# A backbone block on one core: the Strassen sums of the second feed-forward weights made in the loop over f and kept in DRAM

## The chip, the cores and the metric

The kernel runs on one core of a Trainium2 chip. The metric is the device time of one execution in microseconds (us), the median of several runs. A profile of one execution gives the start and duration of every instruction on each engine: TensorE (PE for matmuls, PEld for weight loads), VectorE (DVE), ScalarE (ACT), GpSimd (POOL), and SyncE (SP), which issues nearly all DMA transfers.

## The reference

One transformer-like block for a latent stream x of 1024 tokens and 1024 channels, with a context of 256 tokens: modulation, an input projection, four mixers side by side, an output projection, a residual with layer norm, and then a feed-forward network with its own residual and layer norm. Only the feed-forward network matters here, with D = 1024 and D_FF = 2816:

```python
def swiglu(h, w_in, w_out):
    g, u = jnp.split(h @ w_in, 2, axis=-1)
    return (jax.nn.silu(g) * u) @ w_out
...
        x = layer_norm(ALPHA * x + g2 * swiglu(x * (1.0 + sc2) + sh2, w_ffn_in[l], w_ffn_out[l]), ln2_w[l], ln2_b[l])
```

All data are float32. `w_ffn_out`, 2816 x 1024, holds "the second feed-forward weights".

## The kernel before, in words

**Precision.** An operand of a matmul is split into two parts: a high part, which ScalarE makes by a cast (L853), and a low part, which VectorE makes by subtracting the high part from the value (L854, both in `split2`, called with high priority). Each product is the sum of three matmuls: high by high, high by low, low by high (`PASSES`).

**Strassen.** Both feed-forward matmuls are done by Strassen's scheme in Winograd's form: each matrix is cut into 2 x 2 quarters named 11, 12, 21 and 22, and seven products of quarters, or of sums of quarters called T1 to T4, replace eight. For the second weights T2 = 22 - 12 + 11, T1 = 22 - T2 = 12 - 11, T3 = T2 - 11 = 22 - 12 and T4 = 21 - T2.

**First stage: the loop over f (L1424).** The hidden units come in 22 blocks of 128 (`NFF`). After two passes done without Strassen, nine passes with f = 4, 6, ..., 20 make two blocks each. A pass (`gate_up2`) is two Strassen products: one for the gate, whose results ScalarE puts through SiLU into the tile s, and one for the up projection, whose results VectorE multiplies into s. Each `strassen` loads two 512 KB pieces of first weights into the tiles `raw`, makes the sums of their halves (`a_sums`, L1313) and the parts into tiles `whl`, and runs seven products of 12 matmuls (L1344). VectorE reads and adds the results from PSUM (L1349). At the end of a pass `spill` makes four sums of the quarters of s in a tile S (L1400 to L1403) and stores s and S, 1 MB each, into the DRAM tensor `gd` (L1404, L1405).

**Second stage: seven products over `gd` and the second weights.** For each of the products "11", T2, "21", T1, "22", T3 and T4, in this order, `operands` (L1458) loads chunks of two blocks of 128 rows (the last has one): 512 KB of `gd` into a tile `whl`, and what `weights` (L1442) gives. For "11", "21" and "22" that is one load of 512 KB into `raw`. For T2 it is three loads (two into `raw`, one into `whl`) and two VectorE subtractions or additions of 128x1024 (L1450, L1451); the result stays on chip in three pages for the rest of the kernel. For T1, T3 and T4 it is one load and one subtraction with the kept T2 (L1455). Then both operands are split into high and low parts in tiles that `ring` hands out, and 24 matmuls per chunk run (L1476), 132 in a product. VectorE folds the finished products into the residual rows (L1490 to L1501); T4 accumulates into the PSUM banks that hold T3, after T3 has been read. The rows' last layer norm (`ln2`) and the stores of the output follow.

**Buffers.** `page` is a pool of nine tiles of 8 KB per partition. In the loop over f two of them hold rows of the residual, two the quarter "11" of the first stage's input and two its T4; the others pass between s and S. `page3` is a second pool of eight such tiles. `raw` has two buffers, `whl` four. `ring` gives one chunk in five two tiles of `page` and the other four chunks tiles of `page3`.

**Order of the work.** The code is written as a plain program; a planner at compile time orders the instructions of each engine and of SP's queue by a model of their costs, lets work run ahead when its buffers are free, and prefers what is marked as high priority. At run time each engine and the queue keep that order, and an instruction that waits holds up those behind it.

Of the kernel before, what the change touches and what calls it, by code (L numbers as in the profile page):

```python
# [9 lines left out]
F32 = mybir.dt.float32  # L10
# [4 lines left out]
MUL, ADD, SUB, MAX, MIN = ALU.mult, ALU.add, ALU.subtract, ALU.max, ALU.min  # L15
# [692 lines left out]
NFF = DFF // 128  # L708
# [12 lines left out]
def layout(x):  # L721

    f = np.ascontiguousarray
    g = {n: f(x[n]) for n in ("x", "w_mod", "b_mod", "ln1_w", "ln1_b", "ln2_w", "ln2_b", "mlstm_gate_bias", "s5_glu_w")}
    g["cst"] = const_table()
    kp = lambda a: a.reshape(-1, 128).T
    g["cols"] = f(np.concatenate([kp(x["c"]), kp(x["c_ctx"])] + [kp(x[src][0])[:, k0:k0 + nk] for _, src, k0, nk in VEC], 1))

    st = lambda a: a[0].reshape(2, 8, 2, 64).transpose(2, 3, 0, 1).reshape(128, 16)
    ldt = np.broadcast_to(x["s5_log_dt"][0][:, :, None], (2, 16, 64))[None]  # L730
    bt = [x["s5_b_" + n][0].reshape(8, 2, 64, 16).transpose(1, 2, 0, 3).reshape(128, 128) for n in ("re", "im")]
    ct = [x["s5_c_" + n][0].reshape(8, 2, 16, 64).transpose(1, 3, 0, 2).reshape(128, 128) for n in ("re", "im")]
    dk = np.zeros((128, 8), np.float32)
    dk[0:32] = x["s5_d"][0].reshape(8, 32).T
    g["s5p"] = f(np.concatenate([st(x["s5_a_re"]), st(x["s5_a_im"]), st(ldt)] + bt + ct + [dk], 1))
    g["conv_t"] = f(x["conv_w"][0].reshape(31, 2, 128).transpose(2, 1, 0))
    g["sgu_wt"] = f(x["sgu_w"][0].transpose(2, 0, 1))
    g["sgu_bb"] = f(np.repeat(x["sgu_b"][0].reshape(2, 2, 128).transpose(1, 0, 2), 64, 0))
    g["xt"], g["ct"] = (f(x[n][0].T.reshape(8, 128, -1).transpose(1, 0, 2)) for n in ("x", "ctx"))
    tile_ = lambda w: w.reshape(-1, 128, w.shape[1]).transpose(1, 0, 2)  # L740
    half = lambda w: f(np.stack([tile_(w[0:512]), tile_(w[512:1024])]))
    wi = x["w_in"][0]
    g["wt"] = f(np.stack([tile_(wi[:, c:c + 128]) for _, c in TCOLS]))
    g["wk"], g["wb"] = half(wi[:, 256:512]), half(wi[:, 1296:1552])
    g["wv"] = half(np.concatenate([wi[:, 512:768], wi[:, 1024:1040]], 1))
    g["wm"] = f(x["w_mod"][0][:, 0:2 * D].reshape(4, 2, 128, 2, 2, 512).transpose(4, 0, 2, 1, 3, 5))
    blocks = lambda w: f(w.reshape(8, 128, -1, 128).transpose(2, 1, 0, 3))
    g["w1"] = blocks(x["w_ffn_in"][0])
    g["wo"] = f(x["w_out"][0].reshape(4, 2, 128, 2, 512).transpose(3, 0, 2, 1, 4))
    g["w2"] = f(x["w_ffn_out"][0].reshape(NFF // 2, 2, 128, 2, 512).transpose(1, 3, 2, 0, 4).reshape(4, 128, NFF // 2, 512))  # L750
    return g


# [8 lines left out]
def body(tc, A, out):  # L762
    nc = tc.nc
    v, a, pe, gp = nc.vector, nc.scalar, nc.tensor, nc.gpsimd
    e = Env()
    e.nc, e.tc = nc, tc
    st = ExitStack()
    with st:
# [607 lines left out]
            add(o, u2, W_)  # L1376
            use(1, 0, o)

        def gate_up2(f, B, s):
            def gate(i, h, c):  # L1380
                a.activation(s[:, i, h], c, AF.Silu)

            def up(i, h, c):
                v.tensor_tensor(s[:, i, h], c, s[:, i, h], op=MUL)

            def slot(i, h, spare):
                return pg3.tile([128, 512], F32, name="c12", tag="c12", bufs=1) if spare is None else spare

            strassen(f, B, lambda i, h, spare: s[:, i, h], None, gate)
            strassen(NFF + f, B, slot, None, up)  # L1390

        gd = e.dram.tile([8, 128, NFF // 2, 512], F32, name="gd", bufs=1)

        def spill(f, s):
            k = f // 2
# [24 lines left out]
        next(sums)  # L1423
        for f in range(4, NFF, 2):  # L1424
            s = pair()
            gate_up2(f, B, s)
            spill(f, s)


        NK = NFF // 2  # L1430
        ring = itertools.cycle((page, page3, page3, page3, page3))
        T2 = []

        def w2load(q, k, n, tag="raw"):
            r = sg.tile([128, n, 512], F32, name=tag, tag=tag, bufs=2 if tag == "raw" else 4)
            ld(r, A["w2"][q, :, k:k + n])
            return r

        def t2(k, n):
            return T2[k // 4][:, k % 4:k % 4 + n]  # L1440

        def weights(b, k, n):  # L1442

            if b in ("11", "21", "22"):
                return w2load(("11", "12", "21", "22").index(b), k, n)
            if b == "T2":
                if k % 4 == 0:
                    T2.append(page([128, 4, 512]))
                r, x, y = w2load(3, k, n), w2load(1, k, n), w2load(0, k, n, "whl")
                v.tensor_tensor(r, r, x, op=SUB)  # L1450
                v.tensor_tensor(t2(k, n), r, y, op=ADD)  # L1451
                return t2(k, n)
            r = w2load({"T1": 3, "T3": 0, "T4": 2}[b], k, n)
            x, y = (t2(k, n), r) if b == "T3" else (r, t2(k, n))
            v.tensor_tensor(r, x, y, op=SUB)  # L1455
            return r

        def operands(m, b, k, n):  # L1458
# [120 lines left out]
```

## Time and profile before

| | |
|---|---|
| runs | 1181.01 to 1181.26 us, median 1181.09 of 3 |
| profiled execution | 1180.17 us, its span 1177.6 us |
| mean granted TensorE clock | 0.988 |
| TensorE busy with matmuls | 1135.1 us, 96% of the span |
| VectorE busy | 936.4 us, 80% |
| ScalarE busy | 447.6 us, 38% |
| moved by DMA | 160.57 MB, 136 GB/s over the span |
| second stage, first to last matmul | 945.16 to some 1166.7 us |

Times in the rows are microseconds from the start of the span. A row of a timeline or of the chain of waits gives start, duration, engine, line and operation; in brackets stands how long the engine was idle before it and what ended that. A row of a group gives the count after "x", then the busy time, the mean of one in ns, and the idle time ahead with what ended it. A matmul's duration overlaps the next one's, so the pace is read from starts.

### The profile page before, as it was taken

How to read it: one execution, taken by the hardware profiler on the slowest of the kernel's cores; microseconds unless marked ns; L12 is line 12 of the kernel's file. 1: busy time of each engine (PE TensorE's matmuls, PEld its weight loads, DVE VectorE, ACT ScalarE, POOL GpSimd, SP SyncE). 2: the span in 40 equal slices, each digit the busy share in tenths (PEclk: the TensorE clock that was granted, in tenths of full speed). 3: DMA queues.
4: the chain of work that ended last, by engine and by line, in shares of the span. 5: the costliest groups of instructions: out<-in, count | busy, mean ns of one | idle time of the engine just before them, and what ended most of it. 6: DMA issues, size and time to landing. Idle time of an engine off the chain costs nothing.

```text
span 1177.6 us, 15237 instructions
## 1 busy us (share of the span) xinstructions
PE 1135.1 (96%) x5671; PEld 897.8 (76%) x5671; DVE 936.4 (80%) x1837; ACT 447.6 (38%) x691; POOL 9.6 (1%) x30
## 2 busy tenths in 40 slices
PE   6999999999999999999999999999999989999996
PEld 1487788667888778778887888888888877788875
DVE  7588999988899799889867667675767565897996
ACT  1554444522426334582233333233323242533532
POOL 0010000000000000000000000000000000000000
PEclk9999999999999899999999999999999999999998
DMA  9542111021243346353233143413343387867451
GB/s 361 209 136 84 43 46 57 27 77 63 64 133 109 122 145 199 118 204 108 72 107 122 58 141 110 143 60 119 107 143 106 122 292 266 288 205 275 160 180 71
DMA packets 57484, 160.57 MB, mean 136 GB/s; under 512 B 5378, under 2 KB 9634, under 8 KB 57027
## 3 DMA queue, kind: packets, MB, share of 16 engines
q1 hardware_dynamic: 56994, 158.62, 39.6%
q8 instruction: 44, 0.72, 0.2%
q0 software_dynamic: 272, 0.70, 0.2%
q10 hardware_dynamic: 144, 0.29, 0.1%
q14 instruction: 30, 0.24, 0.1%
HBM read 130.77 MB, written 28.82 MB: 136 GB/s over the span
## 4 chain that ended last, share of the span: by engine, by line
PE 70%; DVE 14%; DMA 9%; issue 3%; ACT 3%; SPq 1%; POOL 0%; DVEq 0%; ACTq 0%; POOLq 0%
PE mm L1344 16%; PE mm L883 12%; PE a L1344 8%; PE mm L1183 5%; PE b L1344 4%; PE b L883 4%; PE a L1476 3%; PE mm L892 3%; DMA raw<-in_w_dram 3%; DMA whl<-gd 3%; PE b L1476 2%; DVE pg L854 2%; PE mm L1476 2%; PE b L564 1%; DVE whl L854 1%
## 5 line engine op out<-in xcount | busy, mean ns | idle before, releaser
L853 ACT CAST whl<-raw 128x512 fp32r<-128x512 f32 (+1 forms) x198 | 121.7, 622 | 279.7 <-PE mm L883 67.2
L883 PE MATMUL mm<-pg,whl 128*128 128x512 f32 x816 | 216.7, 404 | 1.6 <-ACT pg L1206 1.2
L1344 PE MATMUL mm<-pg,whl 128*128 128x512 f32 x864 | 204.8, 389 | 0.0
L1344 PEld LDWEIGHTS mm<-pg,whl 128*128 128x128 f32 x864 | 162.1, 188 | 33.8
L854 DVE TENSOR_TENSOR whl<-raw,whl 128x512 fp32r<-128x512 f32 (+1 forms) x198 | 135.6, 691 | 61.1 <-ACT whl L853 59.2
L883 PEld LDWEIGHTS mm<-pg,whl 128*128 128x128 f32 x816 | 146.5, 188 | 39.3 <-issue 6.1
L1344 PE MATMUL a<-pg,whl 128*128 128x512 f32 x432 | 104.3, 390 | 0.6 <-ACT whl L853 0.6
L1344 PEld LDWEIGHTS a<-pg,whl 128*128 128x128 f32 x432 | 80.9, 188 | 18.2 <-ACT whl L853 1.1
L853 ACT CAST pg<-raw 128x1024 fp32r<-128x1024 f32 (+1 forms) x46 | 45.6, 993 | 78.0 <-DVE raw L1455 44.2
L1476 PE MATMUL a<-pg,pg 128*128 128x512 f32 x210 | 63.6, 399 | 3.6 <-DVE hs L1490 2.3
L854 DVE TENSOR_TENSOR pg<-raw,pg 128x1024 fp32r<-128x1024 f32 (+1 forms) x46 | 52.9, 1153 | 16.4 <-ACT pg L853 16.2
L1476 PE MATMUL mm<-pg,pg 128*128 128x512 f32 x234 | 65.7, 389 | 0.0
L892 PE MATMUL mm<-whl,pg 128*128 128x256 f32 (+1 forms) x448 | 63.1, 288 | 0.0
L1476 PE MATMUL b<-pg,pg 128*128 128x512 f32 x210 | 61.6, 389 | 0.0
L892 PEld LDWEIGHTS mm<-whl,pg 128*128 128x128 f32 x448 | 58.1, 190 | 1.5 <-issue 1.1
L853 ACT CAST pg<-whl 128x1024 fp32r<-128x1024 f32 (+1 forms) x42 | 40.9, 977 | 30.7 <-DMA whl<-gd 28.4
L854 DVE TENSOR_TENSOR pg<-whl,pg 128x1024 fp32r<-128x1024 f32 (+1 forms) x42 | 47.3, 1132 | 6.2 <-ACT pg L853 6.1
L1344 PE MATMUL b<-pg,whl 128*128 128x512 f32 x216 | 51.9, 389 | 0.0
L1476 PEld LDWEIGHTS mm<-pg,pg 128*128 128x128 f32 x234 | 43.9, 188 | 9.1
L1183 PE MATMUL mm<-whl,pg 128*128 128x512 f32 x192 | 50.3, 398 | 0.3 <-DVE pg L1171 0.3
L1183 PE MATMUL mm<-pg 128*128 128x512 f32 x192 | 50.4, 406 | 0.1
L1476 PEld LDWEIGHTS a<-pg,pg 128*128 128x128 f32 x210 | 40.4, 193 | 12.9 <-issue 2.7
(471 smaller groups left out, 1810.2 us busy)
## 6 DMA issues: line engine op xcount, KB each, us to landing
raw<-in_w_dram SPq DMA_DIRECT2D x84, 512.0 KB
gd<-pg SPq DMA_DIRECT2D x22, 1024.0 KB
whl<-gd SPq DMA_DIRECT2D x35, 512.0 KB
pg<-in_wm_dram SPq DMA_DIRECT2D x16, 512.0 KB
raw<-in_wo_dram SPq DMA_DIRECT2D x16, 512.0 KB
raw<-in_wt_dram SPq DMA_DIRECT2D x14, 512.0 KB
mw<-in_w_mod_dram SPq DMA_DIRECT2D x24, 256.0 KB
vx<-in_w_mod_dram SPq DMA_DIRECT2D x24, 256.0 KB
```

Of the source, the lines that this page charges most:

```text
L564: pe.matmul(ps[:, x * 65:(x + 1) * 65], lhsT=D[d][:, x], rhs=vx[:, h, :], start=True, stop=True)
L853: a.copy(hi, r)
L854: v.tensor_tensor(lo, r, hi.bitcast(F32), op=SUB)
L883: pe.matmul(ps[h], lhsT=W(wi, k), rhs=rhs(hi, h, k), **f)
L892: pe.matmul(ps, lhsT=lhs(hi, k), rhs=Ws[k // 4](wi, k % 4), start=(k == 0 and n == 0), stop=(k == 7 and n == 2))
L1183: pe.matmul(ps, lhsT=Yr(hi, half, k)[:, t * 128:(t + 1) * 128], rhs=Ws[k // 2](wi, k % 2), start=(i + n == 0), stop=(i == 7 and n == 2))
L1344: pe.matmul(ps, lhsT=W[:, wi, k, :], rhs=B[b][hi][:, k], start=(first and k + n == 0), stop=(k == 3 and n == 2), skip_group_check=True)
L1476: pe.matmul(ps[t], lhsT=Ag[:, hi, k, t * 128:(t + 1) * 128], rhs=Bg[:, wi, k], start=(first and k0 + k + m == 0), stop=(k0 + k == NK - 1 a ...
```

## The change

The sums of the second weights are no longer made in the second stage. A new input layout `w2k` holds the four quarters of one block k side by side, and `w2_sums(k)` loads them (1 MB) into a page X, makes T3, T1, T2 and T4 from them by four VectorE instructions on 128x512, and stores them (1 MB) into a new DRAM tensor `td`. `gate_up2` calls it between its two halves: for block k = f/2 - 2 in each pass, and in the last two passes (f = 18 and f = 20) also for block k = f/2, which makes eleven blocks. In the second stage `weights` becomes one load for every product, from `td` for T1 to T4 and from `w2` for the others; the three pages of T2, the two extra loads and all subtractions there are gone, and the ring gives two chunks in five tiles of `page`.

```diff
+    g["w2k"] = f(x["w_ffn_out"][0].reshape(NFF // 2, 2, 128, 2, 512).transpose(0, 2, 1, 3, 4).reshape(NFF // 2, 128, 4, 512))
...
-        def gate_up2(f, B, s):
+        def gate_up2(f, B, s, between):
...
             strassen(f, B, lambda i, h, spare: s[:, i, h], None, gate)
+            between()
             strassen(NFF + f, B, slot, None, up)
...
+        td = e.dram.tile([4, 128, NFF // 2, 512], F32, name="td", bufs=1)
+
+        def w2_sums(k):
+            X = page([128, 4, 512])
+            ld(X, A["w2k"][k])
+            v.tensor_tensor(X[:, 3], X[:, 3], X[:, 1], op=SUB)
+            v.tensor_tensor(X[:, 1], X[:, 1], X[:, 0], op=SUB)
+            v.tensor_tensor(X[:, 0], X[:, 3], X[:, 0], op=ADD)
+            v.tensor_tensor(X[:, 2], X[:, 2], X[:, 0], op=SUB)
+            ld(td[:, :, k].rearrange("m p c -> p m c"), X)
...
-            gate_up2(f, B, s)
+            gate_up2(f, B, s, lambda: [w2_sums(k) for k in ((f // 2 - 2,) if f < NFF - 4 else (f // 2 - 2, f // 2))])
...
-        ring = itertools.cycle((page, page3, page3, page3, page3))
-        T2 = []
+        ring = itertools.cycle((page, page3, page, page3, page3))
...
         def weights(b, k, n):
-            if b in ("11", "21", "22"):
-                return w2load(("11", "12", "21", "22").index(b), k, n)
-            if b == "T2":
-                if k % 4 == 0:
-                    T2.append(page([128, 4, 512]))
-                r, x, y = w2load(3, k, n), w2load(1, k, n), w2load(0, k, n, "whl")
-                v.tensor_tensor(r, r, x, op=SUB)
-                v.tensor_tensor(t2(k, n), r, y, op=ADD)
-                return t2(k, n)
-            r = w2load({"T1": 3, "T3": 0, "T4": 2}[b], k, n)
-            x, y = (t2(k, n), r) if b == "T3" else (r, t2(k, n))
-            v.tensor_tensor(r, x, y, op=SUB)
+            r = sg.tile([128, n, 512], F32, name="raw", tag="raw")
+            src = td[("T2", "T1", "T4", "T3").index(b)] if b[0] == "T" else A["w2"][("11", "12", "21", "22").index(b)]
+            ld(r, src[:, k:k + n])
             return r
```

More of the change, by code (lines that the diff above doesn't have):

```diff
@@ L1425, in body @@
             s = pair()
-            gate_up2(f, B, s)
+            gate_up2(f, B, s, lambda: [w2_sums(k) for k in ((f // 2 - 2,) if f < NFF - 4 else (f // 2 - 2, f // 2))])
             spill(f, s)
         NK = NFF // 2
-        ring = itertools.cycle((page, page3, page3, page3, page3))
-        T2 = []
[L1434 to L1440, printed above, removed]
-        def weights(b, k, n):
-            if b in ("11", "21", "22"):
-                return w2load(("11", "12", "21", "22").index(b), k, n)
-            if b == "T2":
-                if k % 4 == 0:
-                    T2.append(page([128, 4, 512]))
-                r, x, y = w2load(3, k, n), w2load(1, k, n), w2load(0, k, n, "whl")
-                v.tensor_tensor(r, r, x, op=SUB)
-                v.tensor_tensor(t2(k, n), r, y, op=ADD)
-                return t2(k, n)
-            r = w2load({"T1": 3, "T3": 0, "T4": 2}[b], k, n)
-            x, y = (t2(k, n), r) if b == "T3" else (r, t2(k, n))
-            v.tensor_tensor(r, x, y, op=SUB)
+        ring = itertools.cycle((page, page3, page, page3, page3))
+        def weights(b, k, n):
+            r = sg.tile([128, n, 512], F32, name="raw", tag="raw")
+            src = td[("T2", "T1", "T4", "T3").index(b)] if b[0] == "T" else A["w2"][("11", "12", "21", "22").index(b)]
+            ld(r, src[:, k:k + n])
             return r
```

## The prediction

> **What bounds the kernel now.** I read the page's first rows, then the busy time by stretches over the loop on f and over each product behind it, then TensorE's timeline around the stretches in which it is not full, and last the chain of waits there.
>
> ```profile
> span 1177.6 us, 15237 instructions
> PE 1135.1 (96%) x5671; PEld 897.8 (76%) x5671; DVE 936.4 (80%) x1837; ACT 447.6 (38%) x691; POOL 9.6 (1%) x30
> ```
>
> TensorE is the bound, so the change can only be worth what TensorE loses in the stages that it touches. In the next fence (stretch, length, busy time with count of PE, PEld, DVE, ACT and POOL, granted clock, DMA share, GB/s) the first row is one pass of the loop over f.
>
> ```profile
> 705.00:743.00 38.00, 38.00 (x169) 31.46 (x169) 25.94 (x40) 12.18 (x20) 0.00 (x0) 1.00 0.31 110
> ...
> 942.00:945.20 3.20, 0.04 (x1) 0.04 (x1) 2.90 (x4) 3.20 (x5) 0.00 (x0) 0.99 0.59 197
> 945.20:950.00 4.80, 4.80 (x14) 3.88 (x15) 4.80 (x7) 0.86 (x1) 0.00 (x0) 0.65 0.84 289
> ...
> 976.00:1012.00 36.00, 32.25 (x134) 25.83 (x133) 21.92 (x22) 13.14 (x16) 0.00 (x0) 0.95 0.81 273
> 1012.00:1042.00 30.00, 30.00 (x134) 24.84 (x133) 27.09 (x30) 14.21 (x15) 0.00 (x0) 1.00 0.82 279
> ...
> 995.00:999.70 4.70, 4.70 (x22) 3.85 (x21) 1.86 (x2) 0.46 (x1) 0.00 (x0) 1.00 0.83 289
> 999.70:1002.80 3.10, 0.65 (x4) 0.20 (x2) 2.50 (x4) 1.63 (x2) 0.00 (x0) 1.00 0.55 156
> 1002.80:1007.30 4.50, 4.50 (x13) 3.56 (x14) 3.76 (x5) 1.36 (x2) 0.00 (x0) 0.62 0.93 320
> ...
> 1132.00:1134.90 2.90, 0.58 (x4) 0.19 (x2) 2.01 (x3) 1.80 (x2) 0.00 (x0) 1.00 0.13 52
> 1134.90:1140.60 5.70, 5.70 (x18) 4.57 (x19) 5.70 (x13) 0.00 (x0) 0.00 (x0) 0.70 0.29 95
> 1140.60:1166.70 26.10, 26.08 (x115) 21.23 (x114) 19.69 (x32) 9.37 (x15) 0.00 (x0) 1.00 0.15 51
> 1166.70:1177.60 10.90, 0.00 (x0) 0.00 (x0) 6.30 (x13) 1.44 (x3) 0.00 (x0) 0.67 0.37 144
> ```
>
> The loop over f keeps TensorE full: nothing can be gained there, only lost. The second stage starts at 945; it holds 7 products of 132 matmuls. At full rate 12 matmuls take 2.72 us (the 849.38 row further on), 0.2267 each, so a product takes 29.92 us. The product that reads "21" (1012 to 1042) runs at that rate; the one that reads T2 (976 to 1012) does not, and the first part of T4 (1134.90 to 1140.60) does not. TensorE's own rows give the exact edges:
>
> ```profile
> 945.16 1.65 PE L1476 MATMUL mm<-pg 128*128 128x512 f32 x3 [3.31 <-ACT pg L853]
> ...
> 976.78 0.62 PE L1476 MATMUL a<-pg,pg 128*128 128x512 f32 x2
> ...
> 994.56 0.74 PE L1476 MATMUL a<-pg,pg 128*128 128x512 f32 x2 [1.30 <-ACT pg L853]
> ...
> 1002.79 0.91 PE L1476 MATMUL a<-pg 128*128 128x512 f32 x2 [2.45 <-ACT pg L853]
> ...
> 1012.70 0.84 PE L1476 MATMUL mm<-pg,pg 128*128 128x512 f32 x3
> ...
> 1131.93 0.61 PE L1476 MATMUL b<-pg 128*128 128x512 f32 x2
> 1134.86 5.73 PE L1476 MATMUL a<-pg,pg 128*128 128x512 f32 x17 [2.32 <-DVE hs L1490]
> ```
>
> **What the change removes: the T2 product.** It runs from 976.78 to 1012.70, 35.92 us, and loses 35.92 - 29.92 = 6.0 us: waits of 1.30 and 2.45 us, and a slow restart, 13 matmuls in 4.50 us where 4.50 / 0.2267 = 19.9 fit (6.9 x 0.2267 = 1.55 us; the clock in that row is 0.62). The chain of waits says what was late:
>
> ```profile
> 985.14 5.64 DMA raw<-in_w_dram
> 990.88 1.24 DVE raw L1450
> 992.15 1.24 DVE pg L1451
> ```
>
> A chunk of two k-blocks takes both raw buffers (w22 and w12), 5.64 + 1.24 + 1.24 = 8.1 us before they can be filled again, while TensorE eats a chunk in 24 x 0.2267 = 5.44 us. It also takes two of the four whl buffers (the operand and w11), so the operand's own load comes late as well. Four loads of 512 KB per 5.44 us would be 385 GB/s, and 320 GB/s at a DMA share of 0.93 is what the 1002.80 row reached. After the change a chunk has two loads, one raw buffer and one whl buffer, and no subtraction: load, cast and low part, about 8 us over two raw buffers, 4 us a chunk against 5.44, at 193 GB/s. That is the traffic of the products "11", "21" and "22" now, and "21" loses nothing. I take back all 6.0 us. Bounds: the two waits without the slow restart, 3.75 us; above, 6.0.
>
> **The subtractions of T1, T3, T4.** The groups of the second stage:
>
> ```profile
> L1455 DVE TENSOR_TENSOR raw<-raw,pg 128x1024 f32<-128x1024 f32 (+1 forms) x12 | 13.4, 1132 | 1.8 <-DMA raw<-in_w_dram 1.8
> L1450 DVE TENSOR_TENSOR raw<-raw 128x1024 f32<-128x1024 f32 (+1 forms) x6 | 6.8, 1136 | 10.9 <-DMA raw<-in_w_dram 10.9
> L1451 DVE TENSOR_TENSOR pg<-raw,whl 128x1024 f32<-128x1024 f32 (+1 forms) x6 | 6.8, 1136 | 1.2 <-DMA whl<-in_w_dram 1.1
> L1455 DVE TENSOR_TENSOR raw<-pg,raw 128x1024 f32<-128x1024 f32 (+1 forms) x6 | 6.7, 1133 | 1.6 <-DMA raw<-in_w_dram 1.6
> ```
>
> VectorE loses 13.4 + 6.8 + 6.8 + 6.7 = 33.7 us of work here. It is worth nothing where TensorE is full, which is everywhere but at the start of T4:
>
> ```profile
> 1130.64 1.15 DVE raw L1455
> 1131.81 1.06 ACT pg L853
> ...
> 1132.89 1.23 DVE L854 TENSOR_TENSOR pg<-raw,pg 128x1024 fp32r<-128x1024 f32 x1 [1.11 <-ACT pg L853]
> 1134.03 1.28 DVE L1490 TENSOR_TENSOR hs<-a,g 128x512 f32<-128x512 f32 x2
> ```
>
> T4 adds into the banks that T3 filled, so TensorE waits until VectorE has read the first of them (L1490, 1134.03). The last matmul of T3 starts at 1131.93 + 0.23; the reading stands behind a low part (1132.89) that waited for a cast, which waited for a T4 subtraction (L1455). With 6.7 us of T3's and half of the 13.4 us (T4's) gone, T4's first operand is done earlier and the reading starts as T3 ends. Of the hole, 1134.86 - (1131.93 + 2 x 0.2267) = 2.48 us, I leave 1.0 (one reading of 0.69 and the hand-over) and take 1.5. The restart then stays fast, as after the 1.30 us wait at 994.56 (22 matmuls in 4.70 us, full rate): the slow one costs 25.1 - 18 = 7.1 matmuls, 1.6 us. Together 3.1 us; bounds 0 (the reading is queued as now) and 2.48 + 1.6 = 4.1.
>
> The Trainium skill, TensorE: Matmul & The Clock Gate, section HAM oscillation, has the clock drop only after idle gaps of over about 3.4 us. Here the clock is 0.62 and 0.70 behind waits of 2.45 and 2.32 us, so the trace disagrees. By the page those slow restarts would not be the gaps' doing and could stay, which is a rival below.
>
> **What it adds: one block of sums in each of nine passes, two in the last two.** Per block one load and one store of 1 MB and four VectorE instructions on 128x512. The rows that price them, with those that show the slack in a pass (the second product of its up half starts at 849.38, so that half at 849.38 - 2.72 = 846.66, and the gate half, 7 products of 2.72 us earlier, at 827.62):
>
> ```profile
> 834.69 21.92 SPq L845 DMA_DIRECT2D raw<-in_w_dram  x4
> ...
> 836.40 0.59 ACT L1381 ACTIVATE pg<-mm 128x512 f32<-128x512 f32 x1
> ...
> 841.59 0.69 DVE L1323 TENSOR_TENSOR raw<-raw 128x512 f32<-128x512 f32 x1 [1.00 <-DMA raw<-in_w_dram]
> ...
> 844.24 0.69 DVE L854 TENSOR_TENSOR whl<-raw,whl 128x512 fp32r<-128x512 f32 x1 [0.77 <-ACT whl L853]
> ...
> 849.38 2.72 PE a L1344 x12
> ...
> raw<-in_w_dram SPq DMA_DIRECT2D x84, 512.0 KB
> gd<-pg SPq DMA_DIRECT2D x22, 1024.0 KB
> ```
>
> VectorE: 4 x 0.69 = 2.8 us on 25.94 of 38, that is 28.7; in the last two passes 5.5, 31.4. It fits beside TensorE. DMA: a pass moves 38 x 110 = 4.2 MB now and 6.3 after, 165 GB/s, half of the 320 above. If this cover were gone, all eleven blocks would be 30 us of VectorE and 11 x 2 x 3.3 = 72 us of transfers (1 MB at 320 GB/s is 3.3 us).
>
> The block's first instruction waits for its load, and VectorE works in order: behind it stand the reading of the banks and the low parts of the next weights. SP issues in order too: behind the block's load, which waits for a page, stand the raw loads of the next half. The weights of the second product of the up half are ready at 844.24 + 0.69 = 844.93 and used at 849.38: 4.45 us of slack. The raw loads go out at 834.69; the pass's s page is first written at 836.40, and the block's page is asked for behind it. So I put the block's load behind those raw loads and its store, some 12 us on, ahead of the next pair: 3.3 us late, within 4.45. Pages: nine, of which two hold rows of the residual, two "11", two T4; s, S and the block share three, and each is stored a pass before it is needed. I take 0.5 us for the loop. Bounds: 0 (TensorE is full, so no gain), and both transfers ahead of one pair of loads in each pass: 6.6 - 4.45 = 2.15 us x 9 = 19.
>
> The Trainium skill, DMA: Bandwidth & Descriptors, says (Queues, rings and completion order) that descriptors of one issuing engine are consumed in ring order on each DMA engine, and (Bandwidth) that 1 MB took 6.15 us in its own measurement. With that figure one transfer ahead of the raw loads would already be 6.15 - 4.45 = 1.7 us late, an estimate of 15 us over nine passes; the 320 GB/s of this trace speaks for 3.3 us.
>
> **The start of the stage and the ring.** The wait of 3.31 us at 945.16 and the slow restart behind it (14 matmuls where 21 fit, 1.6 us) stay: the first operands are loaded into the same buffers. The ring now takes pages for two chunks of five, which the freed T2 pages pay for. 0, with bounds of -3 (VectorE is busy there, 2.90 of 3.20 us, but not by T2) and +6.6 (two blocks' stores ahead of the first loads). The last 10.9 us, behind the last matmul, don't change.
>
> **Sum.** -6.0 - 3.1 + 0.5 + 0 = -8.6 us. The profiled execution took 1180.17 us, 2.6 outside its span of 1177.6, and the median of the runs is 0.92 above it. 1181.09 - 8.6 = 1172.5 us.
>
> **Rivals.** (a) The T4 hole stays: the reading is still behind some low part, since the ring lets operands be prepared further ahead. Then -6.0 + 0.5: 1175.6 us. For it: that VectorE is 100% busy in 1134.90 to 1140.60; against: 33.7 us less work. 0.14. (b) The slow restarts are not the gaps' doing and stay (the page's rule): -(6.0 - 1.55) - 1.5 + 0.5 = -5.45, 1175.6 us. Against it: full rate after 1.30 us, slow after 2.32, 2.45 and 3.31. 0.04. (c) The gain moves to the start: the last pass has two blocks, 4 MB more, just ahead of the first operands, and the first wait grows by 6.6 us: 1179.1 us, no change that can be told. For it: a DMA share of 0.84 from 945.20 to 950; against: the last pass starts at 827.62 + 2 x 38.08 = 903.8, its blocks' loads go out some 9 us on, and with 6.6 us of loads, 5.5 of sums and 6.6 of stores (overlapped) they are stored near 930, while the first operands are cast after 941. 0.11. (d) Slower: the loop over f stalls. The block's load gets in front of the raw loads in SP's queue, or VectorE sits on it, in each pass; from 0.95 us a pass on (8.6 / 9) the gain is gone; at 2.15 us it is 1172.5 - 0.5 + 19 = 1191 us. For it: a wait for raw data of 1.00 us at 841.59 shows loads landing later than their place in VectorE's order allows for; against: 4.45 us of slack and 0.31 DMA share. 0.17. (e) More: VectorE is also freer at the start, the first wait shrinks by 3: 1169.5 us. 0.06.
>
> **Chances.** The forecast has 0.48, so faster is 0.48 + 0.14 + 0.04 + 0.06 = 0.72, no change (within 0.2%, 2.4 us, about what a measurement of this kernel can tell) 0.11, slower 0.17. The range reaches from 1167 (T4's upper bound and (e)) to 1186 (three quarters of (d)'s loss); the forecast's own is 1169 to 1176.
>
> **What would show it.** Right: no wait over 1 us in the product that reads T2, its 132 matmuls in 30 us; under 1.3 us of hole at T4 and clock 1.00 behind it; every pass of the loop still 38.1 us; some 34 us less VectorE work behind the loop and 30 more in it. Wrong: waits of matmuls on L1344 for weights or raw loads in the passes (d), a first wait well over 3.31 us (c), a hole at T4 of 2 us or more (a), or slow stretches without a gap ahead of them (b).

## The result and the profile after

The changed kernel takes 1174.44 us (median of 10 runs, 1167.60 to 1178.07); the kernel before, run beside it on the same chip, takes 1181.17 us (10 runs, 1177.87 to 1185.86). The ratio is 0.9942, with a 95% interval of 0.9920 to 0.9963, so the change is worth 4.4 to 9.4 us. The forecast was 1172.5 us, and the measured median lies within its own range of 1169 to 1176. The profiled execution took 1174.02 us (before: 1180.17).

The page's first two lines, and then the busy time by stretches, with the columns of the prediction (stretch, length, PE, PEld, DVE, ACT, POOL, granted clock, DMA share, GB/s):

```profile
span 1172.2 us, 15295 instructions
...
PE 1133.1 (97%) x5671; PEld 895.4 (76%) x5671; DVE 930.0 (79%) x1851; ACT 445.6 (38%) x691; POOL 9.6 (1%) x30
```

```profile
870.00:908.00 38.00, 36.81 (x163) 30.05 (x162) 29.42 (x47) 11.15 (x20) 0.00 (x0) 1.00 0.59 221
...
980.00:1010.00 30.00, 30.00 (x135) 24.82 (x134) 19.72 (x19) 18.33 (x23) 0.00 (x0) 1.00 0.89 314
...
1130.80:1136.50 5.70, 5.70 (x25) 4.73 (x26) 4.65 (x12) 0.00 (x0) 0.00 (x0) 1.00 0.14 55
```

The first row covers a pass of the loop with two blocks: TensorE is no longer full there (36.81 of 38). The second is the product that reads T2: full. The last is the start of T4: 25 matmuls where 18 ran before, at clock 1.00 where 0.70 was granted. TensorE's own rows after the change give the edges:

```profile
891.23 0.73 PE L1345 MATMUL a<-pg,whl 128*128 128x512 f32 x2 [1.19 <-ACT whl L854]
...
950.08 0.96 PE L1470 MATMUL mm<-pg 128*128 128x512 f32 x3 [2.53 <-ACT pg L854]
...
980.75 0.62 PE L1470 MATMUL a<-pg,pg 128*128 128x512 f32 x2
...
1010.67 0.84 PE L1470 MATMUL mm<-pg 128*128 128x512 f32 x3
...
1129.90 0.61 PE L1470 MATMUL b<-pg 128*128 128x512 f32 x2
1130.76 2.97 PE L1470 MATMUL a<-pg,pg 128*128 128x512 f32 x12 [0.25 <-DVE hs L1484]
```

The T2 product runs from 980.75 to 1010.67, 29.92 us: 132 matmuls at full rate. At T4, 1130.76 - (1129.90 + 2 x 0.2267) leaves a hole of 0.41 us. New are waits of 1.19 us for casts of first weights in the up halves of the last two passes of the loop (the other one at 930.86).

The loss of a stretch, here and below, is the distance between two starts less 0.2267 us for each matmul between them. By stages, from the starts of TensorE's matmuls in the profiled executions (the loop is counted from its first product to the first matmul of the second stage, so the wait ahead of that matmul is in it; the second stage is counted to the start of its last row, of three matmuls):

| us | ahead of the loop | loop | second stage |
|---|---|---|---|
| before | 591.67 | 347.49 | 220.68 |
| after | 592.92 | 351.25 | 210.01 |
| difference | +1.25 | +3.76 | -10.67 |

Ahead of the loop nothing was changed, and this stretch lies between 590.0 and 595.9 us in the profiled executions of all kernels here; its 1.25 us is no effect. The three differences, +0.40 behind the last matmul and -0.09 ahead of the first one make the 5.35 us between the two spans. So the second stage gave more than was expected of it (-6.0 - 3.1 = -9.1) and the loop took more than the +0.5.

Why the loop loses begins in SP's queue. First a pass with one block, then one with two (L846 loads the raw first weights, L1403 the block):

```profile
798.68 0.35 SPq L846 DMA_DIRECT2D raw<-in_w_dram  x1
799.08 0.91 SPq L1403 DMA_DIRECT2D pg<-in_w2k_dram  x1
801.40 0.33 SPq L846 DMA_DIRECT2D raw<-in_w_dram  x1
...
875.89 0.34 SPq L846 DMA_DIRECT2D raw<-in_w_dram  x1
876.28 2.79 SPq L1403 DMA_DIRECT2D pg<-in_w2k_dram  x2
879.18 0.41 SPq L846 DMA_DIRECT2D raw<-in_w_dram  x1
```

The block's load stands between the two raw loads of the up half, not behind them as the prediction had it (in the first pass it leaves ahead of both, at 609.46 against 612.66). In the kernel before, the second raw load of a pass leaves 2.1 to 2.7 us behind the first, first pass aside; the prediction's row at 834.69 counts four loads together and hides that gap. VectorE's rows of the same two passes (L1404 to L1407 are the block's four sums, L1324 and L1325 the sums of the raw weights, L855 their low parts):

```profile
807.17 0.69 DVE L1404 TENSOR_TENSOR pg<-pg 128x512 f32<-128x512 f32 x1 [1.06 <-DMA pg<-in_w2k_dram]
...
809.70 0.68 DVE L1324 TENSOR_TENSOR raw<-raw 128x512 f32<-128x512 f32 x1
...
812.35 1.90 DVE L855 TENSOR_TENSOR whl<-raw,whl 128x512 fp32r<-128x512 f32 x3 [0.17 <-ACT whl L854]
...
883.00 0.69 DVE L1404 TENSOR_TENSOR pg<-pg 128x512 f32<-128x512 f32 x1 [0.40 <-DMA pg<-in_w2k_dram]
...
888.57 0.68 DVE L1324 TENSOR_TENSOR raw<-raw 128x512 f32<-128x512 f32 x1
```

The block's data land first, so its sums are placed ahead of the raw weights' sums. With one block the first low part is done at 812.35 + 0.69 = 813.04, and the product that reads it begins at 813.38:

```profile
813.38 2.88 PE L1345 MATMUL a<-pg,whl 128*128 128x512 f32 x12
```

Of the 4.45 us of slack some 0.3 are left: one block just fits. With two, six sums run ahead of L1324 (two more follow it), and TensorE waits.

The traces' semaphore events tell when the second raw load has landed, counted here from the issue of the first one and without the first pass: 6.1 to 7.0 us in the kernel before, 8.4 to 9.5 with one block between the two, 10.8 and 12.1 with two. VectorE starts L1324 0.1 us behind that landing in the kernel before, and 1.1 to 2.0 us behind it in the changed kernel. So the loop's loss has two parts: the transfers make the raw data late, and VectorE's order adds to it.

### The profile page after: what moved, and what is told of

Read it like the earlier page. It is cut to its first block, busy times and chain, and to the rows that moved or that the text cites. A ratio compares the mean times of both kernels' runs of the same rounds, so it can differ in the third digit from the quotient of the medians.

```text
span 1172.2 us, 15295 instructions
## 1 busy us (share of the span) xinstructions
PE 1133.1 (97%) x5671; PEld 895.4 (76%) x5671; DVE 930.0 (79%) x1851; ACT 445.6 (38%) x691; POOL 9.6 (1%) x30
## 4 chain that ended last, share of the span: by engine, by line
PE 77%; DVE 13%; DMA 4%; issue 4%; ACT 2%; POOL 0%; DVEq 0%; ACTq 0%; POOLq 0%
PE mm L1345 16%; PE mm L884 13%; PE a L1345 8%; PE mm L1470 6%; PE mm L1184 4%; PE b L1345 4%; PE b L884 4%; PE a L1470 3%; PE b L1470 3%; PE mm L893 3%; PE c L1470 2%; PE b L564 1%; DVE whl L855 1%; DVE pg L855 1%; DMA raw<-in_w_dram 1%
## 5 line engine op out<-in xcount | busy, mean ns | idle before, releaser
L855 DVE TENSOR_TENSOR whl<-raw,whl 128x512 fp32r<-128x512 f32 (+1 forms) x198 | 133.6, 689 | 46.3 <-ACT whl L854 44.7
L855 DVE TENSOR_TENSOR pg<-raw,pg 128x1024 fp32r<-128x1024 f32 (+1 forms) x52 | 59.6, 1149 | 20.8 <-ACT pg L854 20.7
L855 DVE TENSOR_TENSOR pg<-whl,pg 128x1024 fp32r<-128x1024 f32 (+1 forms) x42 | 47.4, 1133 | 31.9 <-ACT pg L854 31.6
L854 ACT CAST pg<-raw 128x1024 fp32r<-128x1024 f32 (+1 forms) x52 | 51.5, 992 | 48.9 <-DMA raw<-in_w_dram 18.0
L1470 PE MATMUL mm<-pg,pg 128*128 128x512 f32 x171 | 48.0, 389 | 0.0
L1470 PE MATMUL a<-pg,pg 128*128 128x512 f32 x162 | 47.2, 390 | 0.2 <-DVE hs L1484 0.2
L1470 PE MATMUL b<-pg,pg 128*128 128x512 f32 x162 | 47.1, 389 | 0.0
L1345 PEld LDWEIGHTS b<-pg,whl 128*128 128x128 f32 x216 | 40.5, 188 | 8.4
L1184 PEld LDWEIGHTS mm<-pg 128*128 128x128 f32 x192 | 37.4, 198 | 8.6 <-DVE pg L855 0.7
```

The source lines that it names most:

```text
L854: a.copy(hi, r)
L855: v.tensor_tensor(lo, r, hi.bitcast(F32), op=SUB)
L1184: pe.matmul(ps, lhsT=Yr(hi, half, k)[:, t * 128:(t + 1) * 128], rhs=Ws[k // 2](wi, k % 2), start=(i + n == 0), stop=(i == 7 and n == 2))
L1345: pe.matmul(ps, lhsT=W[:, wi, k, :], rhs=B[b][hi][:, k], start=(first and k + n == 0), stop=(k == 3 and n == 2), skip_group_check=True)
L1470: pe.matmul(ps[t], lhsT=Ag[:, hi, k, t * 128:(t + 1) * 128], rhs=Bg[:, wi, k], start=(first and k0 + k + m == 0), stop=(k0 + k == NK - 1 a ...
```

## The experiments

The edits are against the changed kernel. Each kernel was timed against the kernel before on the same chip; the ratio stands with its 95% interval. The profiles are of one execution each.

**Only the loop's part.** The loop makes and stores the sums, nothing reads them, and the second stage and the ring are those of before.

```diff
-            r = sg.tile([128, n, 512], F32, name="raw", tag="raw")
-            src = td[...] if b[0] == "T" else A["w2"][...]
-            ld(r, src[:, k:k + n])
+            # T2 from three loads and two sums, T1, T3, T4 from one load and T2, as before
```

> The kernel before with the sums added in the loop over f and stored, but not read: the second stage builds its sums as before. It prices the loop alone. My theory: the loop's cost is paid in the first pass and in the two passes with two blocks, where the raw load behind the block's loads makes the second product of the up half wait; about 4 to 5 us slower than before (1185 to 1186), with two waits of about 1.2 us for weights in the last two passes, and the second stage as slow as before. Rival, the loop costs nothing and the start of the stage or the run pays: within 2 us of before, no waits in the loop.

1181.75 us, 1.0010 (0.9987 to 1.0033). The loop's stretch is 353.21 us, with waits of 0.54, 1.19 and 1.80 us in its last three passes; the second stage is 218.99 us, with 5.35 us lost in T2 and a hole of 2.80 us at T4, which has no slow restart behind it here. So the loop costs 5.7 us by this profile, which was this kernel's slowest run, and 1.2 us (-1.5 to +3.9) by the times: the waits are the expected ones, while the times do not exclude the rival's 2 us or less. The gain lies in what the second stage no longer does, not in anything that the loop does to it.

**No sums at all.**

```diff
-            gate_up2(f, B, s, lambda: [w2_sums(k) for k in ...])
+            gate_up2(f, B, s, lambda: None)
...
-            src = td[("T2", "T1", "T4", "T3").index(b)] if b[0] == "T" else A["w2"][...]
+            src = A["w2"][("T2", "T1", "T4", "T3").index(b) if b[0] == "T" else (...).index(b)]
```

> The changed kernel without the sums: T1 to T4 are replaced by plain quarters of the second weights, read from where the others are read, and nothing is added in the loop. It prices the second stage alone. My theory: second stage 10 to 11 us shorter than before and loop as before, so 1169 to 1171. Rival, the loads of the sums from the stored tensor cost something that plain loads do not: then the second stage here is shorter than in the changed kernel (210.0 us from first to last matmul) by 1 us or more.

1168.38 us, 0.9897 (0.9860 to 0.9933). The second stage takes 209.99 us, as long as in the changed kernel (210.01): reading T1 to T4 from `td` costs nothing there. The loop is at 347.58, as before. Against the changed kernel's ratio the sums' work in the loop costs 0.9942 - 0.9897 = 0.45%, some 5 us, with the two intervals allowing for 0.4 to 10.

**The sums on GpSimd.** Only the engine of the four sums is another; SP's order is that of the changed kernel.

```diff
-            v.tensor_tensor(X[:, 3], X[:, 3], X[:, 1], op=SUB)
+            gp.tensor_tensor(X[:, 3], X[:, 3], X[:, 1], op=SUB)
             # and so for the other three
```

> The changed kernel with the four operations of each block on GpSimd in place of VectorE; the order of the transfers on SP's queue is the same. If the waits in the passes with two blocks come from VectorE's order (the block's eight operations stand ahead of the sums of the next weights), they vanish: 2 to 4 us faster than the changed kernel, 1170 to 1172. If they come from the block's loads standing between the two raw loads, they stay at about 1.2 us each, and the time is 1174 or more.

1180.54 us, 0.9991 (0.9972 to 1.0011): the whole gain is gone. The loop takes 359.58 us, and the waits in the two passes with two blocks are still 1.30 and 1.19. Groups of the loop by line, first of the changed kernel, then of this one:

```profile
L1325 DVE TENSOR_TENSOR raw<-raw 128x512 f32<-128x512 f32 x17 | 11.7, 688 | 0.3
```

```profile
L1325 DVE TENSOR_TENSOR raw<-raw 128x512 f32<-128x512 f32 x17 | 20.5, 1207 | 0.6
...
L1404 POOL TENSOR_TENSOR pg<-pg 128x512 f32<-128x512 f32 x11 | 15.1, 1370 | 618.5 <-DMA pg<-in_w2k_dram 585.9
```

GpSimd takes 1.37 us and more for what VectorE does in 0.69 (L1404 in the changed kernel), and VectorE's own sums beside it go from 688 to 1207 ns. So this run does not tell whether VectorE's order makes the loss: it frees VectorE of 30 us and slows it at the same places.

**The loads and stores without the four sums.**

```diff
             ld(X, A["w2k"][k])
-            v.tensor_tensor(X[:, 3], X[:, 3], X[:, 1], op=SUB)
-            # and the other three
             ld(td[:, :, k].rearrange("m p c -> p m c"), X)
```

> The changed kernel without the four VectorE operations of a block: the quarters are loaded and stored as they are, so T1 to T4 are not the sums. The loads stand between the raw loads as in the changed kernel. If the place of the loads is the cause, the waits in the two passes with two blocks stay at 1 us or more each; if VectorE's work is, they vanish and the loop to the second stage takes 348 us: 1171. The second stage is as in the changed kernel, 210 us.

1185.48 us, 1.0047 (1.0029 to 1.0066): with less work it is slower than the kernel before. SP's rows and TensorE's in a pass with two blocks:

```profile
883.88 2.82 SPq L1404 DMA_DIRECT2D td<-pg  x2
886.80 15.71 SPq L846 DMA_DIRECT2D raw<-in_w_dram  x2
```

```profile
895.22 5.49 PE L1345 MATMUL a<-pg,whl 128*128 128x512 f32 x12 [4.13 <-ACT whl L854]
```

Without the sums the stores could go out as soon as the loads had landed, and they were placed ahead of the second raw load as well. That load now leaves 1.4 us ahead of the up half's first matmul, where it left 8.0 us ahead of it in the changed kernel, and TensorE waits 4.13 us (4.24 in the other such pass) with a slow restart of 2.4 to 2.9 us behind it. This is not the sums' cost but SP's order in its plainest form: a store that waits holds the next raw load.

**The block's load alone, between the raw loads, and no sums and no stores.** The second stage reads plain quarters, as in the run with no sums at all.

```diff
             ld(X, A["w2k"][k])
-            # the four sums
-            ld(td[:, :, k].rearrange("m p c -> p m c"), X)
```

> In each pass only the block's load is left, at the place of the changed kernel (between the two raw loads of the up half); its four sums and its store are left out, and the second stage reads plain quarters where it would read T1 to T4, so the sums are no part of what this kernel computes. If the block's transfer alone makes the raw load behind it late, the up halves of the two passes with two blocks still wait about 1.2 us or more, and the first sum of the raw data waits for its DMA: 1171 to 1174 us. If it is the eight sums on VectorE, which stand ahead of the raw data's own, those waits go to under 0.4 us and the time is that of the kernel without any sums, 1167 to 1170 us (0.9897 of before).

1170.22 us, 0.9916 (0.9899 to 0.9933): on the border of the two expected times, and not to be told from the run with no sums at all. In the two passes with two blocks the up half loses 0.66 and 0.69 us in place of 1.55 and 1.56, and 0.28 us of that at the product that waited 1.19 us in the changed kernel, which is what the second expectation said. VectorE's row and TensorE's there:

```profile
884.01 0.69 DVE L1324 TENSOR_TENSOR raw<-raw 128x512 f32<-128x512 f32 x1
```

```profile
886.21 3.26 PE L1345 MATMUL a<-pg,whl 128*128 128x512 f32 x12
```

The raw load lands as late as in the changed kernel (10.7 and 12.2 us behind the issue of the first), and L1324 follows a reading of a bank without a wait for its load. So the transfers use up the slack but cost no more than the 0.66 and 0.69; the other 0.9 us a pass come with the sums on VectorE and the stores behind them, which no run separates.

**The block behind the up half.** Loads, sums and stores are those of the changed kernel.

```diff
-            between()
             strassen(NFF + f, B, slot, None, up)
+            between()
```

> The changed kernel with the block of sums made behind the up half of a pass and not between the halves, which puts the block's load behind both raw loads in SP's queue. If the loads between the raw loads are what stalls the last two passes, the waits of 1.19 us at their up halves are gone, and the loop to the start of the second stage takes 348 to 349 us (351.25 in the changed kernel, 347.49 before): 1171 to 1173. Rival, VectorE is too full in the passes with two blocks: a wait of 1 us or more stays in each of them, 1174 or more. The first wait of the second stage may grow, as the last two blocks now end closer to it.

1167.61 us, 0.9897 (0.9877 to 0.9916): faster than the changed kernel, and level with the kernel that makes no sums. SP's rows, VectorE's and TensorE's, the first two kinds from the first pass with two blocks, the last from the start of the second stage:

```profile
873.23 2.38 SPq L846 DMA_DIRECT2D raw<-in_w_dram  x2
875.65 0.90 SPq L1403 DMA_DIRECT2D pg<-in_w2k_dram  x2
```

```profile
880.67 0.69 DVE L1324 TENSOR_TENSOR raw<-raw 128x512 f32<-128x512 f32 x1 [1.51 <-DMA raw<-in_w_dram]
```

```profile
939.34 2.88 PE L1345 MATMUL mm<-pg,whl 128*128 128x512 f32 x12
942.22 0.73 PE L1470 MATMUL mm<-pg 128*128 128x512 f32 x2
```

Both raw loads now leave ahead of the block's, L1324 is first on VectorE and the eight sums come behind it; the passes with two blocks lose 0.43 us at most. In the first pass the block's load still leaves ahead of both raw loads (606.83 against 610.03), and its up half loses 2.11 us as in the changed kernel (2.15; before the change 1.23). The wait at the start of the second stage has gone too: 942.22 - 939.34 = 2.88 us for 12 matmuls that take 2.72. The trace shows the order of the first loads of that stage changed as well (the load from `gd` leaves ahead of a raw one, and not behind two); that this is why the wait went is argued, not shown. The loop takes 346.02 us, less than before the change, since that wait was counted in it: without the wait its passes lose 3.1 us, where 5.8 are lost in the changed kernel and 1.3 before the change.

**Only the loop's part, behind the up half.** The edit of the first experiment and that of the one just above together.

> The kernel before with the loop's part of the change alone (loads, sums, stores into the new tensor, which nothing reads; the second stage makes T2 and the subtractions as before), but with the block called behind the up half. If the loop's cost lies only in the place of the block's load, the stretch from the loop's first product to the second stage is 345 to 348 us (347.49 before, 353.21 with the block between the halves) and the time is within 2 us of before; the waits in T2 and the hole at T4 stay. If the block's work costs time wherever it stands, the stretch is 350 us or more and the time 3 to 6 us above before.

1179.23 us, 0.9981 (0.9964 to 0.9999). The loop's stretch is 345.29 us and the second stage 221.37, with waits of 1.46 and 2.67 us in T2 and 2.65 at T4. Here too the first wait of the second stage has gone: the loop's last 12 matmuls start at 942.00 and the second stage at 944.79.

The passes lose 2.5 us, where 1.3 were lost before the change, and 0.9 of the difference is in the first pass, where the block's load is again ahead of both raw loads. So all eleven blocks, 22 MB of transfers and 30 us of VectorE, cost the passes 1.2 us in this place, and the wait that went makes up for more than that.

**The block's load on ScalarE's queue.**

```diff
-            ld(X, A["w2k"][k])
+            nc.scalar.dma_start(X, A["w2k"][k])
```

> The changed kernel, but the block's load (L1403) is issued from ScalarE's queue in place of SP's; point in the program, sums and store as before. If the raw loads are late because the block's load stands ahead of one of them in SP's queue, then the waits of 1.19 us in the up halves of the two passes with two blocks go to under 0.3 us, and the stretch from the loop's first product to the second stage is about 347 us (351.25 in the changed kernel): 1169 to 1172 us. If it is the transfers that take the raw loads' time, wherever they are issued, the waits stay over 1 us and the time at 1174 to 1176. If ScalarE, which now has to wait for the block's page, holds its casts back, waits on casts come up in all eleven passes or parts of them, and the time is above 1178 us.

1184.37 us, 1.0039 (1.0016 to 1.0062), and none of the three expectations describes it. ScalarE, VectorE and TensorE in a pass with one block:

```profile
849.52 0.33 ACTq L1403 DMA_DIRECT2D pg<-in_w2k_dram  x1
```

```profile
857.03 0.69 DVE L1324 TENSOR_TENSOR raw<-raw 128x512 f32<-128x512 f32 x1 [2.41 <-DMA raw<-in_w_dram]
857.64 0.68 DVE L1350 TENSOR_TENSOR pg<-hs,mm 128x512 f32<-128x512 f32 x1
```

```profile
858.47 5.71 PE L1345 MATMUL mm<-pg,whl 128*128 128x512 f32 x24 [1.05 <-DVE pg L1350]
```

SP issues its raw loads one behind the other again, but the block's megabyte runs at the same time on the other queue, and the raw data come late, 8.3 to 10.8 us behind the issue of the first raw load in all passes but the first: VectorE waits 2.41 us for them at L1324, the reading of a bank (L1350) stands behind it, and TensorE waits for that bank. This comes up in eight passes, 0.8 to 2.9 us each: 363.24 us for the loop. Another queue does not take the block out of the raw load's way.

**One block in every pass.** The last two blocks are made behind the two passes ahead of the loop, so no pass has two.

```diff
         spill(0, s)
+        w2_sums(9)
...
         spill(2, s)
+        w2_sums(10)
...
-            gate_up2(f, B, s, lambda: [w2_sums(k) for k in ((f // 2 - 2,) if f < NFF - 4 else (f // 2 - 2, f // 2))])
+            gate_up2(f, B, s, lambda: w2_sums(f // 2 - 2))
```

> The changed kernel with one block of sums in each of the nine passes; the two others are made behind the two passes ahead of the loop. If 2 MB between two raw loads is more than the 4.45 us of slack and 1 MB is not, the waits of 1.19 us in the last two passes vanish and none comes in their place: 2.7 us less in the loop, 1171 to 1172. Rival, the start of the loop, where VectorE is fuller, pays instead: the loop to the start of the second stage stays at 351 us or the stretch ahead of it grows by over 2 us.

1175.59 us, 0.9961 (0.9938 to 0.9984): no better than the changed kernel. The waits in the last two passes have gone, and blocks meet the raw loads of the loop's first pass, where the second raw load leaves behind a block's load and another block's store and lands 11.6 us behind the issue of the first:

```profile
624.67 1.65 PE L1345 MATMUL a<-pg,whl 128*128 128x512 f32 x3 [4.86 <-ACT whl L854]
```

**T2 on chip, T1, T3 and T4 from `td`.** T2 is built in the second stage with three loads and two sums as before; no other subtraction is left there.

```diff
         def weights(b, k, n):
+            if b == "T2":
+                # three loads, r - x, then + y, into a kept page, as before
```

> The changed kernel, but the product that reads T2 takes its operand as before (three loads, two VectorE operations, pages), while T1, T3 and T4 come from the stored sums. My theory (four loads a chunk and both raw buffers a chunk are the cause of the 6.0 us): the waits in that product come back, 5 to 6 us, and the hole at T4 stays closed: 1179 to 1181. Rival, the T2 gain came from VectorE work or the ring: less than 3 us come back.

1182.30 us, 1.0002 (0.9981 to 1.0023). The second stage takes 221.01 us. T2 has waits of 0.33, 1.54 and 1.47 us and loses 4.22 us, somewhat less than was expected, and against the expectation the hole of T4 is back, though the subtractions of T1, T3 and T4 have gone. ScalarE's row in T3 and TensorE's at T4:

```profile
1105.53 0.62 ACT L854 CAST pg<-raw 128x512 fp32r<-128x512 f32 x1 [7.76 <-DMA raw<-td]
```

```profile
1138.89 5.37 PE L1483 MATMUL a<-pg,pg 128*128 128x512 f32 x12 [3.71 <-DVE hs L1497]
```

The casts of T3 wait for their loads here. In the changed kernel the casts of the same chunk start with a wait for TensorE to give a tile of the ring back, which means that the operands are ahead:

```profile
1092.47 0.62 ACT L854 CAST pg<-whl 128x512 fp32r<-128x512 f32 x1 [3.43 <-PE c L1470]
```

This run keeps the ring of the changed kernel, which takes more tiles of `page`, while three tiles of it go to T2 again. That the shortage of pages, and not T2's loads, brings the hole back is a rival that this run does not exclude.

**T2 from `td`, the other subtractions as before.** T2 is loaded into pages that are kept; T1, T3 and T4 are one load and one subtraction each; the ring is that of before.

```diff
         def weights(b, k, n):
+            if b == "T2":
+                # one load from td into a kept page
+            if b[0] == "T":
+                # one load and one subtraction with the kept T2, as before
```

> The changed kernel, but T2 alone comes from the stored sums, into three pages that are kept, and T1, T3 and T4 are subtracted from it in the second stage as before, with the ring of before. It tells what closed the hole at the start of T4. If it was the subtractions of T1, T3 and T4 (my prediction), the hole of 2.3 us and the slow restart come back: second stage 213 to 215 us, 1178. If it was the lead over TensorE that the loads of the T2 product lost and never won back, the hole stays at 1 us or less and the second stage takes 210 to 211 us: 1174 to 1175.

1175.57 us, 0.9963 (0.9947 to 0.9979); second stage 212.11 us. T2 loses nothing, and of T4's hole 1.36 us are left, without a slow restart (0.22 us lost behind it):

```profile
1132.86 3.42 PE L1485 MATMUL a<-pg,pg 128*128 128x512 f32 x14 [1.20 <-DVE hs L1499]
```

The two runs belong together. With T2 alone relieved, T4's loss goes from 2.48 + 1.74 (hole and restart, before) to 1.36 + 0.22, though the other subtractions are still there; with everything but T2 relieved, on the ring of the changed kernel, it does not go at all. The last step, from a hole of 1.36 to the 0.41 of the changed kernel, comes with the other subtractions and the ring, whose share the next run puts at 0.1 us.

**The ring of before.**

```diff
-        ring = itertools.cycle((page, page3, page, page3, page3))
+        ring = itertools.cycle((page, page3, page3, page3, page3))
```

> The changed kernel, but the operands' pages come in the order of the kernel before (room for one chunk in five in the pages of the loop over f, in place of two). If it is VectorE's and the loads' smaller work that closes the waits of T2 and the hole at T4, the second stage stays at 210 to 211 us and the time at 1173 to 1176 us. If the closing hangs on the operands being prepared further ahead, the hole at T4 comes back (1.2 to 2.5 us and a slow restart), the second stage is 212 to 215 us and the time 1176 to 1180 us.

1175.20 us, 0.9956 (0.9942 to 0.9970); second stage 211.18 us, T2 without a loss, a hole of 0.54 us at T4. The new ring's share is too small to be told from none.

## Why the prediction was right, and where it was not

**T2: right, in size and in where it comes from.** -6.0 us was forecast; the product takes 29.92 us in place of 35.92, the run in which T2 alone was relieved lost nothing there, and the run in which T2 alone was made on chip lost 4.22. Which of the extra loads, the two raw buffers and the two sums held it back was not separated; in the prediction's group rows L1450 waits 10.9 us for loads, which speaks for the loads.

**T4: right in size, wrong in the step.** -3.1 us was forecast (bounds 0 and -4.1); the loss, hole and restart, went from 4.22 to 0.50 us, -3.7. The prediction's step was that T3's and T4's subtractions leave VectorE's queue and so the reading comes up sooner. With those subtractions in place and T2 relieved, 1.58 of the 4.22 us are left; with the subtractions gone and T2 built on chip, TensorE waits 3.71 us at the hole (with the ring's rival named there). So T2 mattered more than what stands next to the hole. That it did so because the second stage fell behind in T2 and never got ahead again is argued from the casts of T3, which wait for TensorE in the changed kernel and for loads in that run; why the loads from `td` come as late there as the 7.76 us shows stays open. Of the 3.7 us, the 1.7 of the slow restart are no steady price: in the two runs with the loop's part alone the hole is 2.80 and 2.81 us, and only 0.34 and 0.51 us are lost behind it (the last section says why).

**The loop: the term that was mis-sized.** +0.5 us was forecast (bounds 0 and +19). From the first to the last product of the loop it is +4.5 us by the two profiles: 3.1 in the up halves of the two passes with two blocks, 0.9 in the first pass and 0.5 in the others. By the times of the runs it is 1 to 5 us (1.2 from the loop's part alone, 5 from leaving the sums out). The step that failed is "I put the block's load behind those raw loads". It was placed between them, and rival (d), which named this, had the right mechanism with the wrong reach: in the passes with one block the 4.45 us of slack hold, in the two with two they do not. The price in that step, 3.3 us late for a megabyte, was no underestimate: the second raw load lands on average 2.3 us later with one block than in the same passes before the change, and 4.7 and 5.2 us later with two. What the step left out is VectorE's order, 1.1 to 2.0 us from that landing to L1324.

The block's own load takes longer than 3.3 us: it leaves at 799.08 and its first sum waits until 807.17, 8.1 us, with two raw loads and the store of S under way as well. The Trainium skill's 6.15 us for 1 MB (DMA: Bandwidth & Descriptors, Bandwidth) is nearer to that, but the 15 us that the prediction worked out from it did not come, since six of the nine passes lose 0.34 us at most.

VectorE's added work was sized rightly: the four sums take 30.2 us over the loop (7.5 or 7.6 for each of the four lines), where 30 were forecast.

**The start of the stage: 0 forecast, -1.7 in the profile.** The wait is 2.53 us in place of 3.31, and the product behind it loses 0.75 us, where 1.70 were lost. It is not a steady gain: the kernels with the ring of before, with T2 alone relieved, and without sums wait 3.00, 2.85 and 3.04 us. Rival (c), that the gain would move here, did not come.

**The sum.** -6.0, -3.7 and -1.7 make -11.4; the loop gives 4.5 back, and the 1.25 us ahead of the loop and 0.3 at the two ends stand against it: -5.35 in the profiles, -6.7 between the medians. The forecast's -8.6 came near since the terms on the gaining side were 2.3 us too small and the loop's 4.0, so that the closeness of the sum is in part luck; the largest term, T2, was not. The lower end of the wide range, 1167, does not come out of the terms that the prediction names for it: 1172.5 - 1.0 - 3 is 1168.5.

## What to carry to other kernels

Work that fits by its busy time is cheap or dear by where its load stands in the issuing queue, and by what its place there puts in front on the engine that uses the data. Count what is issued between two loads that a matmul waits for, and place new transfers behind the last of them; the same eleven blocks cost the passes 4.5 us with their loads between the raw loads, and 1.2 and 1.8 us in the two runs with ten of them behind. A hole late in a stage can be the debt of an earlier product: ask where the supply lost its lead before changing what stands next to the hole.

## What the runs showed of the hardware

**GpSimd beside VectorE.** A 128x512 float32 sum took GpSimd 1.37 to 1.60 us on average, and a VectorE sum of the same size with both inputs on chip (L1325) took 1207 ns beside it in place of 688. The Trainium skill (SBUF — State Buffer, Who interferes with whom) says that a VectorE instruction with two inputs in SBUF contends with a GpSimd instruction that reads SBUF, over a shared pair of ports that is an exclusive lock. The longer mean of L1325 agrees.

**The clock after a wait.** How long TensorE had waited does not tell whether it restarts slowly. In the run with the loop's part alone the clock is 0.62 in the 4.4 us behind a wait of 1.84 us (1010.42) and 1.00 in the 4.0 us behind one of 2.64 (1142.79). The changed kernel has 1.00 behind 2.53 us, where the kernel before had 0.62 behind 2.45. Neither the rule that the prediction read from its own rows (fast after 1.30, slow after 2.32) nor one threshold of 3.4 us fits.

The clock records of the traces show why. The granted clock is 0.50 or 1.00 (other values are means over a stretch), and within one profile all its changes lie on one grid of 3.41 us, whose place differs between profiles. Three stretches of that grid at the hole of T4, first in the kernel before, then in the run with the loop's part alone (TensorE's busy time behind the length, granted clock third from the end):

```profile
1132.88:1136.30 3.42, 1.44 (x6) 1.24 (x7) 3.41 (x4) 0.92 (x1) 0.00 (x0) 1.00 0.29 81
1136.30:1139.71 3.41, 3.41 (x9) 2.67 (x8) 3.41 (x10) 0.00 (x0) 0.00 (x0) 0.50 0.20 77
1139.71:1143.12 3.41, 3.41 (x16) 2.80 (x15) 3.41 (x5) 1.86 (x2) 0.00 (x0) 1.00 0.00 0
```

```profile
1137.72:1141.14 3.42, 2.43 (x11) 1.69 (x9) 2.31 (x3) 1.40 (x2) 0.00 (x0) 1.00 0.71 235
1141.14:1144.55 3.41, 1.76 (x8) 1.49 (x9) 3.41 (x5) 0.59 (x1) 0.00 (x0) 1.00 0.42 101
1144.55:1147.97 3.42, 3.42 (x17) 2.84 (x16) 3.42 (x11) 0.00 (x0) 0.00 (x0) 1.00 0.15 58
```

In the first, 1.98 us of idle time fall into one stretch, and the next one runs at 0.50. In the second, an edge splits a longer wait into 0.99 and 1.65 us, and the clock stays at 1.00. From 590 us to the last matmuls the fourteen profiles hold 2354 such stretches at full clock. TensorE was idle for at least 0.58 of 18 of them, and the next one ran at 0.50 each time; behind the 2334 in which it was idle for less than 0.53 that never happened; of the two in between one was followed by 0.50, and the changed kernel's 2.53 us (0.55) is the other. The Trainium skill (TensorE: Matmul & The Clock Gate, What's actually happening) has the clock follow activity in a free-running window of 3.4 us, so that the same gap can fall either way; the grid agrees.
